# 128-row matmuls throughout the prompt's attention, and paged attention with late sums, split softmax steps and unnormalised exponentials of both maps

## The chip, the core and the metric

The program runs on one NeuronCore of a Trainium2 chip. The metric is the device time of one execution in microseconds (us). The engines are TensorE (PE in the rows; PEld is its weight load), VectorE (DVE), ScalarE (ACT), GpSimd (POOL) and SyncE (SP), which here only issues DMAs. Each engine runs its own queue in order; semaphores join them.

## What is computed

One decoder layer runs for a prompt of 1024 tokens behind 16 learned meta tokens, and for eight single-token samples with 4096 cached tokens each. Its attention is differential: four heads, each with two softmax maps of 64 columns over values of 128 columns, an ALiBi bias and causal masking. Beside it stands a convolution group of width 31. Both go into one output projection, and a SwiGLU network of 2816 hidden columns follows. Everything is float32.

```python
def diff_attend(q, k, v, q_pos, k_pos, lam, slopes):
    s = einsum('bqhjd,bkhjd->bhjqk', q, k) * HEAD_DIM ** -0.5
    s = s - slopes * (q_pos[:, None] - k_pos[None, :])
    s = where(k_pos <= q_pos, s, NEG_INF)
    p = softmax(s, axis=-1)
    a = p[:, :, 0] - lam * p[:, :, 1]
    return einsum('bhqk,bkhe->bqhe', a, v)
# sample: the same over cache_k[page_table], cache_v[page_table] (32 pages of 128
# tokens per sample) and the sample's own new key and value
```

## The kernel before

Products that must be exact are made of three matmuls (`mm3`, lines 147 to 149): each operand is split into a rounded part H and a remainder L, and HH, HL and LH are added in PSUM. The program is written as one stream, which a planner orders by priority on a simulated time line; the pools' buffers are given out by that planner, and an instruction waits for a buffer until its last reader is done.

*Prompt.* The input projection comes in stripes of 128 columns: the convolution's eight, then per head a stripe each of v, q and k (`stripe_v`, `stripe_q`, `stripe_k`), whose chunks are emitted between the attention blocks of the head before. `attn(h, i)` takes head h and query block i of 128 rows, over W = 16 + 128(i+1) keys. For each map j a score tile is made of two matmuls (lines 498 and 499): the first has 128 rows, with q's rounded 64 rows and their remainders stacked (`L1`) against k's rounded rows twice (`R1`); the second has q's rounded 64 rows against k's remainder `R2`, 64 rows. VectorE adds the bias and takes the maximum (line 500), ScalarE the exponential (508), VectorE combines the maps (516), TensorE transposes blocks (524), ScalarE copies them out (527), and TensorE multiplies by v (538). Key tile 0 holds the 16 meta tokens: its transpose has 16 columns and its product 16 rows (`vm`). The convolution runs on VectorE and GpSimd behind the first attention blocks. The tiles of 1056 columns (`slab`) share 35 buffers.

*Samples.* `dec_units` is a generator that is stepped at set points of the prompt's code, from block 3 of the attention on. A key unit loads two pages (`page_pair`, line 649, on SP), GpSimd multiplies them by the query (664), VectorE sums each 64 columns into the scores (668). A value unit loads two pages and multiplies them by the weights `a` on TensorE (716), four pages side by side in four column groups. Key units run ahead of value units by `lag`, and from then on two and two. When the 16 key units of a batch are out, `dec_softmax` follows at once: bias, maximum, an all-reduce over the partitions on GpSimd (686), subtraction, exponential, sum, a second all-reduce (692), reciprocal, scaling, and the two maps into one, `a` (700). `dec_values` begins with the sample's own value (706). The page tiles have four buffers of a tag `kv`, and after attention six more of a tag `p`, which then serve six of every seven pairs. Each page's DMA is placed in SP's queue behind the latest matmul of the prompt, by order alone.

```python
yield from keys(per + cfg["lag"])     # lag=2 key units ahead of the values
...
for b in range(DB):
    for n in dec_values(b, st):       # stops after each value unit
        yield
        yield from keys(n)            # as many key units after a group of value units
```

After attention comes the output projection, then the feed-forward network (`ffn`): gate and up (`pg`, `pu`) and down (`dn`, line 974 adds each of its 128x512 tiles into `y` on VectorE). Score, gate, up and down tiles share six PSUM buffers. `fill` steps the sample's work between those blocks. When the last values are out, `sample_units` sums the four column groups from `pvD` (line 1093) and runs the samples' output projection and feed-forward network.

Of the kernel before, what the change touches and what calls it, by code (L numbers as in the profile page):

```python
# [16 lines left out]
P = 128  # L17
# [28 lines left out]
def tile_layer(ctx: ExitStack, tc: tile.TileContext, I, O, cfg):  # L46
# [70 lines left out]
    pvD = dr.tile([DB, 4, NH, 512], F32, name="pvD")  # L117
# [166 lines left out]
    def stripe_k(h):  # L284
        HL = w_in_split(4 + h)
        R1s = [slab(f"R1_{h}{j}", F32R) for j in range(2)]
        R2 = slab(f"R2_{h}", F32R)
        k = slab(f"kT{h}")
        heads[h].update(R1=R1s, R2=R2)
# [29 lines left out]
    def stripe_v(h):  # L319
        HL = w_in_split(8 + h)  # L320
        vT = slab(f"vT{h}")
        for c, o in proj(HL, f"pv{h}"):
            key_evac(vT, o, c, 8 + h, "s")
            if c < 2:
                yield
        v = slab(f"V{h}")
        heads[h] = {"V": v}
        for pt, ts, name in key_tiles(vT, f"vn{h}"):
            for t0, nj, rows, c in key_runs(ts):
                dst = vm[:, h * P : (h + 1) * P] if t0 == 0 else v[:, (t0 - 1) * P : (t0 - 1 + nj) * P]  # L330
                S.copy(dst, pt[:rows, c * P : (c + nj) * P])
        D.dma_start(nvp[META:, h, :].rearrange("(j p) d -> p j d", j=NB), kn(v))
        yield

    def v_out():
        D.dma_start(nvp[0:META].rearrange("t h d -> t (h d)"), vm)
# [139 lines left out]
    def attn(h, i):  # L476
# [8 lines left out]
        L1s, R1s, R2 = heads[h]["L1"], heads[h]["R1"], heads[h]["R2"]  # L485
# [6 lines left out]
        for j in range(2):  # L492
            p = slp.tile([P, NKEY], F32, tag="p", name=f"p{h}{i}{j}", bufs=cfg["p"])
            sl = slice(j * HD, (j + 1) * HD)
            for a in range(0, W, w):
# [3 lines left out]
                T.matmul(o, lhsT=L1s[j][sl, qs], rhs=R2[sl, a:e], start=False, stop=True)  # L499
# [35 lines left out]
        for st, ts in ats:  # L535
            for n, t in enumerate(ts):
                w = KT[t][1]
                x = T.matmul(  # L538
                    o[:, oc], lhsT=st[:w, n * P : (n + 1) * P], rhs=vtile(h, t),
# [39 lines left out]
    mTs = cst.tile([P, 8, DB], F32, name="mTs")  # L579

# [74 lines left out]
    def dec_scores(b, st):  # L655
# [4 lines left out]
        for pg in range(0, NPG, 2):  # L660
            kt = page_pair(ck, b, pg, f"k{b}_{pg}")
            n = b * NPG // 2 + pg // 2
            eng = V if cfg["dve_mul"] and n % cfg["dve_mul"] == 0 else G
            eng.tensor_tensor(kt, kt, qB.unsqueeze(1).to_broadcast([P, 2, 512]), op=ALU.mult)  # L664
            for g in ((pg, pg + 1) if n < cfg["ksp"] else (slice(pg, pg + 2),)):
                src = kt if isinstance(g, slice) else kt[:, g - pg : g - pg + 1, :]
                g = g if isinstance(g, slice) else slice(g, g + 1)
                V.tensor_reduce(  # L668
                    s[:, g, :].rearrange("p a c -> p (a c)"),
                    src.rearrange("p a (c d) -> p (a c) d", d=HD), axis=AX.X, op=ALU.add,  # L670
                )
            yield b

    def dec_softmax(b, st):
# [7 lines left out]
        sv = s.rearrange("p g c -> p c g")  # L682
        m = smt(f"dm{b}", 8, 2)
        V.tensor_reduce(m, sv, axis=AX.X, op=ALU.max)
        mg = smt(f"dg{b}", 8, 2)
        G.partition_all_reduce(mg, m, P, bass.bass_isa.ReduceOp.max)
        V.tensor_tensor(s, s, mg.unsqueeze(1).to_broadcast([P, NPG + 1, 8]), op=ALU.subtract)
        S.activation(s, s, AF.Exp)
        l = smt(f"dl{b}", 8, 2)
        V.tensor_reduce(l, sv, axis=AX.X, op=ALU.add)  # L690
        lg = smt(f"dk{b}", 8, 2)
        G.partition_all_reduce(lg, l, P, bass.bass_isa.ReduceOp.add)
        co = smt(f"dc{b}", 8, 2)
        V.reciprocal(co, lg)
        cov = co.rearrange("p (h j) -> p h j", j=2)
        V.tensor_scalar(cov[:, :, 1], cov[:, :, 1], neglam, None, op0=ALU.mult)
        V.tensor_tensor(s, s, co.unsqueeze(1).to_broadcast([P, NPG + 1, 8]), op=ALU.mult)
        a = dec.tile([P, NPG + 1, NH], F32, tag="a", name=f"a{b}")
        s4 = s.rearrange("p g (h j) -> p (g h) j", j=2)
        V.tensor_tensor(a.rearrange("p g h -> p (g h)"), s4[:, :, 0], s4[:, :, 1], op=ALU.add)  # L700
        st[b] = a

    def dec_values(b, st):
        a = st.pop(b)
        pv = pdec(f"pv{b}")
        T.matmul(pv[0:NH, :], lhsT=a[:DB, NPG, :], rhs=nat["v"], start=True, stop=False)
        vs = []
        for pg in range(0, NPG, 2):
# [3 lines left out]
            if len(vs) == size:  # L712
                for q, vt in vs:
                    for i in range(2):
                        g = (q + i) % 4
                        x = T.matmul(  # L716
                            pv[32 * g : 32 * g + NH, :], lhsT=a[:, q + i, :], rhs=vt[:, i, :],
                            start=(q + i < 4 and g > 0), stop=q + i >= NPG - 4, tile_position=(0, 32 * g),
# [3 lines left out]
                vs = []  # L722
            yield 0 if vs else size
        pvs = dec.tile([P, 512], F32, tag="gs", name=f"pvs{b}", bufs=2)
        for g in range(4):
            S.copy(pvs[32 * g : 32 * g + NH, :], pv[32 * g : 32 * g + NH, :])
            D.dma_start(pvD[b, g], pvs[32 * g : 32 * g + NH, :])

    def dec_units():
        st = {}  # L730
        ks = (b for bb in range(DB) for b in dec_scores(bb, st))
        nk, ready = 0, 0
        per = NPG // 2

        def softmaxes():
            nonlocal ready
            while "k" in nat and ready < nk // per:
                dec_softmax(ready, st)
                ready += 1

        def keys(n):
            nonlocal nk
            for _ in range(n):
                if nk < DB * per:
                    next(ks)
                    nk += 1
                    softmaxes()
# [5 lines left out]
        softmaxes()  # L753
# [331 lines left out]
    def sample_units():  # L1085
        og = slab("og")
        og2 = slab("og2")
        for g in range(4):
            D.dma_start(
                (og, og2)[g // 2][:DB, (g % 2) * 512 : (g % 2) * 512 + 512].rearrange("b (h e) -> b h e", h=NH),  # L1090
                bass.AP(tensor=pvD.tensor, offset=pvD.offset + g * NH * 512, ap=[[4 * NH * 512, DB], [512 + P, NH], [1, P]]),
            )
        V.tensor_tensor(og[:DB, :1024], og[:DB, :1024], og2[:DB, :1024], op=ALU.add)
        o = og[:DB, 0:512]
        V.tensor_tensor(o, o, og[:DB, 512:1024], op=ALU.add)
# [243 lines left out]
    lag=2,  # L1339
# [46 lines left out]
```

## Time and profile before

| | us |
|---|---|
| median of three timed runs | 1557.42 (1555.67 to 1562.95) |
| the profiled execution | 1566.71 |
| its span, first to last instruction | 1564.9 |
| TensorE busy in the span | 1441.4 |
| VectorE, ScalarE, GpSimd busy | 932.0, 517.9, 561.9 |

In the profile a busy TensorE includes the time in which one matmul holds up the next; how far apart two of them start is read from the timeline. Behind an idle time stands what ended it; "issue" means that nothing of the profile was waited for. The granted clock of TensorE is 1 at 2.4 GHz and 0.5 at 1.2 GHz; a stretch shows the mean. In a matmul's row 64*128 is the weights' rows by columns, and behind it stand the moving rows and columns. Lines are those of the kernel before.

### The profile page before, as it was taken

What the parts mean: (1) busy time and instruction counts of PE and PEld (TensorE: products, weight loads), DVE (VectorE), ACT (ScalarE), POOL (GpSimd) and SP (SyncE); (2) the same over time, 40 slices, a digit from 0 to 9 for tenths busy, and PEclk for the clock granted to TensorE, in tenths of its full rate; (3) what the DMA queues carried; (4) which work ended last, traced back from release to release, by engine and by line L of the source; (5) the groups of instructions that cost most, each with busy time, mean ns of one, the idle gap of its engine ahead of it and who ended that gap; (6) DMA issues with size and microseconds to landing.
All of it is one profiled execution on the core that took longest, in us unless ns stands there. A gap on an engine that the chain in (4) does not pass through costs nothing.

```text
span 1564.9 us, 21652 instructions
## 1 busy us (share of the span) xinstructions
PE 1441.4 (92%) x6974; PEld 1080.5 (69%) x6974; DVE 932.0 (60%) x1519; ACT 517.9 (33%) x1023; POOL 561.9 (36%) x351
## 2 busy tenths in 40 slices
PE   6999999999869999989796996979979999999996
PEld 5998778888636787667474674756757677566665
DVE  5789987866545567565564745535545527454247
ACT  6566655586435334213112020111112121212121
POOL 3698735325224213444452533525445100000013
PEclk9999899999857999999898997999989999999999
DMA  8202113315405547668575664766767765764464
GB/s 261 60 12 57 37 58 95 108 59 166 142 0 168 185 152 248 202 215 270 184 250 173 202 215 157 242 195 205 240 189 232 238 219 178 262 200 142 155 210 163
DMA packets 199119, 264.03 MB, mean 169 GB/s; under 512 B 16119, under 2 KB 99384, under 8 KB 198997
## 3 DMA queue, kind: packets, MB, share of 16 engines
q1 hardware_dynamic: 199005, 262.64, 51.4%
q8 instruction: 55, 0.90, 0.2%
q14 instruction: 59, 0.48, 0.1%
HBM read 245.85 MB, written 17.22 MB: 168 GB/s over the span
## 4 chain that ended last, share of the span: by engine, by line
PE 74%; DVE 10%; issue 6%; DMA 4%; POOL 3%; SPq 2%; ACT 1%; POOLq 0%; DVEq 0%; ACTq 0%
PE pg L147 6%; PE pg L149 6%; PE pg L148 6%; PE pu L147 5%; PE pu L148 5%; PE pu L149 5%; PE pv L716 4%; PE dn L147 4%; PE dn L148 3%; PE dn L149 3%; PE o L538 3%; PE S L499 2%; PE mo L149 2%; PE mo L148 2%; PE mo L147 2%
## 5 line engine op out<-in xcount | busy, mean ns | idle before, releaser
L664 POOL TENSOR_TENSOR k<-k,qB 128x1024 f32<-128x1024 f32 x128 | 318.8, 2505 | 343.9 <-DMA k<-in_cache_k 247.3
L668 DVE TENSOR_REDUCE s<-k 128x16 f32<-128x1024 f32 x128 | 155.1, 1214 | 153.6 <-POOL k L664 153.5
L147 PE MATMUL dn<-wH,aH 128*128 128x512 f32 x352 | 144.3, 412 | 28.5 <-DVE y L974 28.5
L931 ACT CAST wH<-wr 128x1024 fp32r<-128x1024 f32 x66 | 69.2, 1048 | 300.0 <-DVE wL L933 151.9
L147 PE MATMUL pu<-hH,wH 128*128 128x512 f32 x352 | 141.3, 401 | 4.2 <-DVE y L972 4.2
L148 PE MATMUL dn<-wL,aH 128*128 128x512 f32 x352 | 143.8, 408 | 0.0
L149 PE MATMUL dn<-wH,aL 128*128 128x512 f32 x352 | 142.6, 405 | 0.0
L933 DVE TENSOR_TENSOR wL<-wr,wH 128x1024 fp32r<-128x1024 f32 x66 | 106.1, 1608 | 60.2 <-ACT wH L931 23.5
L147 PE MATMUL pg<-hH,wH 128*128 128x512 f32 x352 | 141.2, 401 | 0.0
L148 PE MATMUL pu<-hL,wH 128*128 128x512 f32 x352 | 140.7, 400 | 0.0
L149 PE MATMUL pu<-hH,wL 128*128 128x512 f32 x352 | 140.5, 400 | 0.0
L149 PE MATMUL pg<-hH,wL 128*128 128x512 f32 x352 | 139.9, 398 | 0.0
L148 PE MATMUL pg<-hL,wH 128*128 128x512 f32 x352 | 139.6, 397 | 0.0
L404 POOL TENSOR_TENSOR cb<-cb 128x512 f32<-128x512 f32 x80 | 101.8, 1305 | 21.2 <-ACT cb L403 12.1
L147 PEld LDWEIGHTS dn<-wH,aH 128*128 128x128 f32 x352 | 68.6, 195 | 59.1 <-DVE y L974 35.4
L974 DVE TENSOR_TENSOR y<-dn,y 128x512 f32<-128x512 f32 x144 | 95.9, 683 | 21.2 <-PE dn L149 20.8
L413 DVE SCALAR_TENSOR_TENSOR acc<-u,cw,acc 128x512 f32<-128x512 f32 x144 | 99.3, 749 | 0.3
L950 DVE TENSOR_TENSOR sg<-sg,pu 128x512 f32<-128x512 f32 x44 | 30.0, 682 | 107.6 <-PE pu L149 107.5
L147 PEld LDWEIGHTS pu<-hH,wH 128*128 128x128 f32 x352 | 67.1, 191 | 29.1 <-issue 11.9
L148 PEld LDWEIGHTS dn<-wL,aH 128*128 128x128 f32 x352 | 68.8, 195 | 25.5 <-issue 10.3
L147 PEld LDWEIGHTS pg<-hH,wH 128*128 128x128 f32 x352 | 66.4, 189 | 28.6 <-issue 12.5
L957 ACT CAST aH<-sg 128x512 fp32r<-128x512 f32 x44 | 27.3, 621 | 175.5 <-DVE sg L950 175.4
(571 smaller groups left out, 3008.8 us busy)
## 6 DMA issues: line engine op xcount, KB each, us to landing
k<-in_cache_k SPq DMA_DIRECT2D x256, 256.0 KB
v<-in_cache_v SPq DMA_DIRECT2D x256, 256.0 KB
wr<-in_w_gate SPq DMA_DIRECT2D x22, 512.0 KB
wr<-in_w_up SPq DMA_DIRECT2D x22, 512.0 KB
wr<-in_w_down SPq DMA_DIRECT2D x22, 512.0 KB
sd<-in_w_down SPq DMA_DIRECT2D x22, 512.0 KB
sw_gate<-in_w_gate SPq DMA_DIRECT2D x20, 512.0 KB
sw_up<-in_w_up SPq DMA_DIRECT2D x20, 512.0 KB
```

What stands on the lines that cost most here:

```text
L147: T.matmul(out, lhsT=wH, rhs=xH, start=first, stop=False)
L148: T.matmul(out, lhsT=wH, rhs=xL, start=False, stop=False)
L149: mark(T.matmul(out, lhsT=wL, rhs=xH, start=False, stop=last))
L404: G.tensor_tensor(accp, accp, t, op=ALU.add)
L413: V.scalar_tensor_tensor(dst, src, cw[:, ct, k : k + 1], acc, op0=ALU.mult, op1=ALU.add)
L538: x = T.matmul(o[:, oc], lhsT=st[:w, n * P : (n + 1) * P], rhs=vtile(h, t), start=t == 0, stop=t == nt - 1,)
L664: eng.tensor_tensor(kt, kt, qB.unsqueeze(1).to_broadcast([P, 2, 512]), op=ALU.mult)
L668: V.tensor_reduce(s[:, g, :].rearrange("p a c -> p (a c)"), src.rearrange("p a (c d) -> p (a c) d", d=HD), axis=AX.X, op=ALU.add,)
L716: x = T.matmul(pv[32 * g : 32 * g + NH, :], lhsT=a[:, q + i, :], rhs=vt[:, i, :], start=(q + i < 4 and g > 0), stop=q + i >= NPG - 4, tile ...
L931: S.copy(H[:, :1024], raw[:, :1024])
L933: V.tensor_tensor(L[:, :1024], raw[:, :1024], H[:, :1024].bitcast(F32), op=ALU.subtract)
L974: V.tensor_tensor(y[b][:, ws], o, y[b][:, ws], op=ALU.add)
```

## The change

Prompt: `R2` becomes two tiles of 128 rows, the key's remainder stacked twice, so that the second score matmul has 128 rows: it multiplies all of `L1`, and so adds the product of both remainders too. VectorE writes the second half of each. Key tile 0 is transposed 128 columns wide, its 16 rows are copied into one of three tiles whose other rows are zero, and `vm` has 128 rows, zero below the 16th.

Samples: a key unit's sum is emitted behind the product of the next key unit (`rlag`; an order, no semaphore). The softmax is split: bias, maximum and one all-reduce when the batch's sums are out (`dec_max`), subtraction and exponential two key units later (`dec_exp`, `elag`), sums over the pages amid the values (`dec_total`). The exponentials are not divided by their sums; both maps go to the value matmuls as eight columns. The sums over partitions, the reciprocals, the sample's own value and the difference of the maps follow once for all batches in `sample_units`. `lag` is 7 instead of 2.

```diff
     def stripe_k(h):
-        R2 = slab(f"R2_{h}", F32R)
+        R2s = [slab(f"R2_{h}{j}", F32R) for j in range(2)]
...
-                (G if cfg["r2_g"] else V).tensor_tensor(R2[sl, d], k[sl, d], R1s[j][sl, d].bitcast(F32), op=ALU.subtract)
+                (G if cfg["r2_g"] else V).tensor_tensor(R2s[j][sl, d], k[sl, d], R1s[j][sl, d].bitcast(F32), op=ALU.subtract)
+                V.tensor_tensor(R2s[j][ot, d], k[sl, d], R1s[j][sl, d].bitcast(F32), op=ALU.subtract)
...
-    vm = cst.tile([META, AW], F32, name="vm")
+    vm = cst.tile([P, AW], F32, name="vm")
+    G.memset(vm, 0.0)
+    metas = [cst.tile([P, P], F32, name=f"metaT{x}") for x in range(3)]
+    for x in metas:
+        G.memset(x, 0.0)
...
-                T.matmul(o, lhsT=L1s[j][sl, qs], rhs=R2[sl, a:e], start=False, stop=True)
+                T.matmul(o, lhsT=L1s[j][:, qs], rhs=R2s[j][:, a:e], start=False, stop=True)
...
-                k0, w = KT[t]
-                T.transpose(out=pt[:w, n * P : (n + 1) * P], in_=A[:, k0 : k0 + w], identity=ident)
+                k0 = KT[t][0]
+                T.transpose(out=pt[:, n * P : (n + 1) * P], in_=A[:, k0 : k0 + P], identity=ident)
...
-                S.copy(st[:rows, c * P : (c + nj) * P], pt[:rows, c * P : (c + nj) * P])
+                dst = metas[(h * NB + i) % 3][:rows, :] if t0 == 0 else st[:rows, c * P : (c + nj) * P]
+                S.copy(dst, pt[:rows, c * P : (c + nj) * P])
...
-                    o[:, oc], lhsT=st[:w, n * P : (n + 1) * P], rhs=vtile(h, t),
+                    o[:, oc], lhsT=metas[(h * NB + i) % 3] if t == 0 else st[:, n * P : (n + 1) * P], rhs=vtile(h, t),
...
     def dec_scores(b, st):
-            eng.tensor_tensor(kt, kt, qB.unsqueeze(1).to_broadcast([P, 2, 512]), op=ALU.mult)
-            for g in ((pg, pg + 1) if n < cfg["ksp"] else (slice(pg, pg + 2),)):
-                V.tensor_reduce(s[:, g, :]..., src..., axis=AX.X, op=ALU.add)
+            x = G.tensor_tensor(kt, kt, qB.unsqueeze(1).to_broadcast([P, 2, 512]), op=ALU.mult)
+            products.append((s[:, pg : pg + 2, :], kt))
+            if len(products) > cfg["rlag"]:
+                head_sums(x)
...
+    def head_sums(after):
+        s, kt = products.pop(0)
+        x = V.tensor_reduce(
+            s.rearrange("p a c -> p (a c)"), kt.rearrange("p a (c d) -> p (a c) d", d=HD), axis=AX.X, op=ALU.add
+        )
+        if after is not None:
+            tc.add_manual_dep(x.ins, after.ins.name, behind, reason="sums behind a later product")
...
+    def dec_exp(b, st):
+        s, mg = st[b]
         V.tensor_tensor(s, s, mg.unsqueeze(1).to_broadcast([P, NPG + 1, 8]), op=ALU.subtract)
         S.activation(s, s, AF.Exp)
-        V.tensor_reduce(l, sv, axis=AX.X, op=ALU.add)
-        G.partition_all_reduce(lg, l, P, bass.bass_isa.ReduceOp.add)
-        V.reciprocal(co, lg)
-        V.tensor_scalar(cov[:, :, 1], cov[:, :, 1], neglam, None, op0=ALU.mult)
-        V.tensor_tensor(s, s, co.unsqueeze(1).to_broadcast([P, NPG + 1, 8]), op=ALU.mult)
-        V.tensor_tensor(a.rearrange("p g h -> p (g h)"), s4[:, :, 0], s4[:, :, 1], op=ALU.add)
+        st[b] = s
+
+    def dec_total(b, s):
+        V.tensor_reduce(dsum[:, b, :], s.rearrange("p g c -> p c g"), axis=AX.X, op=ALU.add)
+        V.tensor_tensor(selfa, selfa, s[:DB, NPG, :], op=ALU.add)
...
     def dec_values(b, st):
-        T.matmul(pv[0:NH, :], lhsT=a[:DB, NPG, :], rhs=nat["v"], start=True, stop=False)
-                            pv[32 * g : 32 * g + NH, :], lhsT=a[:, q + i, :], rhs=vt[:, i, :],
+                            pv[32 * g : 32 * g + 8, :], lhsT=a[:, q + i, :], rhs=vt[:, i, :],
...
+            if pg == NPG // 2:
+                dec_total(b, a)
...
+        def softmaxes(all_=False):
+            while "k" in nat and ready < (nk - len(products)) // per:
+                dec_max(ready, st)
+                at.append(nk)
+                ready += 1
+            while exped < ready and (all_ or nk >= at[exped] + cfg["elag"]):
+                dec_exp(exped, st)
+                exped += 1
...
     def sample_units():
+        ogs = [slab(f"og{g}") for g in range(4)]        # eight DMAs from pvD
+        tot = pdec("dtot")
+        T.matmul(tot[:DB, : DB * 8], lhsT=ones, rhs=dsum.rearrange("p b c -> p (b c)"), start=True, stop=True)
+        V.tensor_tensor(mine, tot..., own, op=ALU.mult)
+        V.tensor_reduce(co, mine..., axis=AX.X, op=ALU.add)
+        V.reciprocal(co, co)
+        for g in range(1, 4):
+            V.tensor_tensor(o2, o2, ogs[g][:DB, :1024], op=ALU.add)
+        for j in range(2):                              # own value, sum, scaling: 512 columns each
+            V.tensor_tensor(t, nat["v"]..., w..., op=ALU.mult)
+            V.tensor_tensor(hv(ogs[0], j), hv(ogs[0], j), t, op=ALU.add)
+            V.tensor_tensor(hv(ogs[0], j), hv(ogs[0], j), cov[:, :, j]..., op=ALU.mult)
...
-    lag=2,
+    lag=7, rlag=1, elag=2,
```

## Rows read from the trace of the kernel before

**Rows 1.** Page, part 1: busy time of each engine.
```profile
PE 1441.4 (92%) x6974; PEld 1080.5 (69%) x6974; DVE 932.0 (60%) x1519; ACT 517.9 (33%) x1023; POOL 561.9 (36%) x351
```

**Rows 2.** Stretches: busy PE, PEld, DVE, ACT, POOL; granted TensorE clock, DMA share, GB/s.
```profile
150.00:200.00 50.00, 41.02 (x198) 35.17 (x197) 48.74 (x97) 32.02 (x69) 40.03 (x33) 0.85 0.11 32
200.00:400.00 200.00, 194.41 (x1134) 165.48 (x1134) 148.69 (x348) 125.63 (x319) 79.19 (x54) 0.97 0.30 94
400.00:505.00 105.00, 85.62 (x325) 55.29 (x324) 49.97 (x155) 44.38 (x111) 30.84 (x18) 0.66 0.33 110
505.00:1240.00 735.00, 673.48 (x3001) 483.10 (x3000) 419.88 (x500) 159.90 (x266) 287.43 (x139) 0.95 0.64 209
```

**Rows 3.** Waits of TensorE: us in total, times, longest.
```profile
PE dn L147 <- DVE y L974: 28.5, 8, 7.6
PE pv L706 <- DVE a L700: 28.4, 4, 13.9
PE S L498 <- DVE mx L500: 14.7, 4, 10.2
```

**Rows 4.** Timeline of TensorE in attention: start, us, what.
```profile
282.12 0.40 PE L498 MATMUL S<-R,L 128*128 128x328 f32 x1
282.45 0.41 PE L499 MATMUL S<-R,L 64*128 64x328 f32 x1
...
289.02 0.34 PE L149 MATMUL pq<-xH,wi2L 128*128 128x384 f32 x1
289.20 0.34 PE L147 MATMUL pq<-xH,wi2H 128*128 128x384 f32 x1
...
414.82 0.70 PE L499 MATMUL S<-R,L 64*128 64x400 f32 x1
415.45 0.70 PE L498 MATMUL S<-R,L 128*128 128x400 f32 x1
...
500.22 0.48 PE L538 MATMUL o<-vm,ats 16*128 16x128 f32 x2
500.63 0.94 PE L538 MATMUL o<-V,ats 128*128 128x128 f32 x6
```

**Rows 5.** Timeline of GpSimd around one all-reduce.
```profile
855.13 0.43 POOL L692 PARTITION_ALL_REDUCE dk<-dl  x1 [5.91 <-issue]
862.63 9.56 POOL L664 TENSOR_TENSOR k<-k,qB 128x1024 f32<-128x1024 f32 x4 [7.07 <-issue]
```

**Rows 6.** Waits of VectorE: us in total, times, longest.
```profile
DVE s L668 <- POOL k L664: 153.5, 53, 12.1
...
DVE dc L694 <- POOL dk L692: 32.2, 7, 12.6
```

**Rows 7.** Score matmuls of 64 rows (line 499) in two stretches.
```profile
400.00:414.00 14.00, 5.80 (x14) 2.66 (x14) 0.99 0.32 96
414.00:499.00 85.00, 16.24 (x25) 6.84 (x24) 0.58 0.33 111
```

**Rows 8.** VectorE groups with two SBUF inputs: by form; durations min/median/max.
```profile
L876 DVE TENSOR_TENSOR mL<-mx,mH 128x384 fp32r<-128x384 f32 x8 | 6.6, 828 | 6.7 <-ACT mH L875 6.7
...
L700 DVE TENSOR_TENSOR a<-s x8: 286/291/2508, 449.1 to 1234.6; 128x132 f32<-128x132 f32 x8
```

**Rows 9.** Group of line 706.
```profile
L706 PE MATMUL pv<-natv,a 8*4 8x512 f32 x16 | 11.5, 809 | 28.4 <-DVE a L700 28.4
```

**Rows 10.** Waits of the DMA queue on SP: us in total, times, longest.
```profile
SPq L649 <- DVE s L668: 67.8, 14, 14.7
...
SPq L130 <- PE S L499: 36.5, 2, 22.0
```

**Rows 11.** Timeline of VectorE at the sample's first sum.
```profile
1284.31 1.21 DVE L1093 TENSOR_TENSOR og<-og,og 8x1024 f32<-8x1024 f32 x1 [7.18 <-DMA og<-pvD]
```

**Rows 12.** GpSimd group of the key products, 505 to 1240.
```profile
L664 POOL TENSOR_TENSOR k<-k,qB 128x1024 f32<-128x1024 f32 x108 | 271.3, 2527 | 308.2 <-DMA k<-in_cache_k 218.5 <-issue 62.9 <-DMA v<-in_cache_v 10.5
```

More of the change, by code (lines that the diff above doesn't have):

```diff
@@ L116, in tile_layer @@
     qsD = dr.tile([DB, AW], F32, name="qsD")
[L117 removed]
+    pvD = dr.tile([DB, 4, 8, 512], F32, name="pvD")
     def rstd_of(ssq, rows, inv_n, name, w=1, add=EPS):
@@ L579, in tile_layer @@
     mTs = cst.tile([P, 8, DB], F32, name="mTs")
+    selfa = cst.tile([DB, 8], F32, name="selfa")
+    G.memset(selfa, 0.0)
+    dsum = cst.tile([P, DB, 8], F32, name="dsum")
+    ones = cst.tile([P, DB], F32, name="ones")
+    G.memset(ones, 1.0)
+    own = cst.tile([DB, DB, 8], F32, name="own")
+    G.memset(own, 1.0)
+    G.affine_select(
+        out=own, in_=own, pattern=[[-1, DB], [0, 8]], compare_op=ALU.is_equal, fill=0.0, base=0, channel_multiplier=1
+    )
     def dec_consts():
@@ L716, in dec_values @@
                         x = T.matmul(
-                            pv[32 * g : 32 * g + NH, :], lhsT=a[:, q + i, :], rhs=vt[:, i, :],
-                            start=(q + i < 4 and g > 0), stop=q + i >= NPG - 4, tile_position=(0, 32 * g),
+                            pv[32 * g : 32 * g + 8, :], lhsT=a[:, q + i, :], rhs=vt[:, i, :],
+                            start=q + i < 4, stop=q + i >= NPG - 4, tile_position=(0, 32 * g),
                         )
@@ L731, in dec_units @@
         ks = (b for bb in range(DB) for b in dec_scores(bb, st))
-        nk, ready = 0, 0
+        nk, ready, exped, at = 0, 0, 0, []
         per = NPG // 2
[L735 to L738, printed above, removed]
+        def softmaxes(all_=False):
+            nonlocal ready, exped
+            while "k" in nat and ready < (nk - len(products)) // per:
+                dec_max(ready, st)
+                at.append(nk)
                 ready += 1
+            while exped < ready and (all_ or nk >= at[exped] + cfg["elag"]):
+                dec_exp(exped, st)
+                exped += 1
         def keys(n):
@@ L746, in keys @@
                     nk += 1
-                    softmaxes()
+                    if nk == DB * per:
+                        while products:
+                            head_sums(None)
+                    softmaxes(nk == DB * per)
                     yield
@@ L1094, in sample_units @@
-        o = og[:DB, 0:512]
-        V.tensor_tensor(o, o, og[:DB, 512:1024], op=ALU.add)
+            for j in range(2):
+                D.dma_start(
+                    ogs[g][:DB, j * 512 : j * 512 + 512].rearrange("b (h e) -> b h e", h=NH),
+                    bass.AP(
+                        tensor=pvD.tensor, offset=pvD.offset + (g * 8 + j) * 512,
+                        ap=[[4 * 8 * 512, DB], [2 * 512 + P, NH], [1, P]],
+                    ),
+                )
+        tot = pdec("dtot")
@@ new lines, in sample_units @@
+        T.matmul(tot[:DB, : DB * 8], lhsT=ones, rhs=dsum.rearrange("p b c -> p (b c)"), start=True, stop=True)
+        mine = smt("dmine", DB * 8, 1)[:DB].rearrange("p (b c) -> p b c", b=DB)
+        V.tensor_tensor(mine, tot[:DB, : DB * 8].rearrange("p (b c) -> p b c", b=DB), own, op=ALU.mult)
+        co = smt("dco", 8, 1)[:DB]
+        V.tensor_reduce(co, mine.rearrange("p b c -> p c b"), axis=AX.X, op=ALU.add)
+        V.reciprocal(co, co)
+        cov = co.rearrange("p (h j) -> p h j", j=2)
@@ new lines, in sample_units @@
+        V.tensor_scalar(cov[:, :, 1], cov[:, :, 1], neglam[:DB], None, op0=ALU.mult)
+        o2 = ogs[0][:DB, :1024]
+        for g in range(1, 4):
+            V.tensor_tensor(o2, o2, ogs[g][:DB, :1024], op=ALU.add)
+        hv = lambda t, j: t[:DB, j * 512 : j * 512 + 512].rearrange("b (h e) -> b h e", h=NH)
+        for j in range(2):
+            t, w = hv(ogs[1], j), selfa.rearrange("p (h j) -> p h j", j=2)[:, :, j]
+            V.tensor_tensor(
+                t, nat["v"].rearrange("b (h e) -> b h e", h=NH), w.unsqueeze(2).to_broadcast([DB, NH, P]), op=ALU.mult
+            )
+            V.tensor_tensor(hv(ogs[0], j), hv(ogs[0], j), t, op=ALU.add)
+            V.tensor_tensor(
+                hv(ogs[0], j), hv(ogs[0], j), cov[:, :, j].unsqueeze(2).to_broadcast([DB, NH, P]), op=ALU.mult
+            )
@@ L1096, in sample_units @@
+        o = ogs[0][:DB, 0:512]
+        V.tensor_tensor(o, o, ogs[0][:DB, 512:1024], op=ALU.add)
         ov = o.rearrange("b (h e) -> b h e", h=NH)
```

44 lines of the change are left out of this document (12 added, 32 removed).

## The prediction

> **What bounds the kernel now.** I read the page first, then a table of busy time over stretches, then TensorE's waits, and only then the timeline. TensorE is busy for 92% of the span [rows 1], so its time is what counts, but the stretches differ [rows 2]. From 150 to 200 VectorE is busy for 48.7 of 50 us and TensorE for 41: the convolution's taps bound it. From 200 to 400 TensorE is busy for 194 of 200 us. From 400 to 505, the end of attention, it is busy for 85.6 of 105 us at a mean granted clock of 0.66. From 505 to 1240, the feed-forward network with the paged attention beside it, it idles for 735 - 673.5 = 61.5 us at a mean clock of 0.95. The list of waits names VectorE at each large idle time [rows 3]: `dn` blocks wait for `y` sums (28.5 us), the value matmuls for the weights `a` (28.4), a score matmul for a row maximum (10.2 of 14.7 in one wait).
>
> Two things lie beneath. In attention a score matmul of 328 columns with 128 rows is followed 0.33 us later by its partner of 64 rows; two projection matmuls of 384 columns, all with 128 rows, stand 0.18 us apart at the same full clock, 2.4 GHz [rows 4]. So a change of row count between neighbours costs about as much again as the matmul. In the paged part GpSimd stands idle for 5.91 us before an all-reduce and for 7.07 us before the product after it, though neither waits for data [rows 5]. VectorE's queue is in order, so it stands behind that: 153.5 us for products, 32.2 for the second all-reduce of a batch [rows 6].
>
> **128 rows everywhere.** There are 112 pairs of score matmuls: 25 between 414 and 499, mostly at 1.2 GHz [rows 7], the other 87 mostly at 2.4. Full clock: 0.33 us apart now; 328 columns without the change of rows are 0.18 x 328/384 = 0.15; 174 x 0.18 = 31 us. Half clock: 0.63 apart for 400 columns, twice 0.18 without, so 50 x 0.28 = 14 us. The 16-row meta pair holds TensorE for 0.41 us [rows 4]; a plain matmul of 128 columns is at most the 0.18 of 384 and at least its third, 0.06; I take 0.12, so 32 blocks x 0.17 = 5 us. Together 50 us of TensorE time. The 16-column transposes become 128 wide, 32 x 0.06 = 2 us at most by the same ends; I take 0.
>
> What of this is on the path? Between 150 and 200 nothing, VectorE sets the end there. Between 200 and 400 lie about 60 pairs and 18 blocks, 22 + 3 = 25 us, but VectorE's 148.7 us stand close behind. It gets the new subtractions, six a head, 24 in all. The nearest form, `mL`, 384 columns and two SBUF inputs, takes 0.83 us on the mean [rows 8]. So 18 x 0.83 = 15 us come here, and VectorE stands at 164 of the 175 us that TensorE would leave. I take 16 of the 25. The six subtractions of head 0 fall where VectorE is the bound: +5. The ends for all 24: the 132-column add of `a` takes 0.29 us on the median and 2.51 at most, beside products of 2.4 [rows 5, 8]: 7 and 60 us.
>
> The Trainium skill's SBUF — State Buffer (section "SBUF: two separate sides") speaks against this edit: a VectorE instruction with two SBUF inputs and a GpSimd instruction shut each other out for the whole instruction. The slowest add of `a` agrees. If each of the 24 subtractions met a product of 2.4 us, the rule would add 58 us to the sum; by the row's median it adds nothing.
>
> **The end of attention, 400 to 505.** 14 pairs at full clock, 25 at half and eight meta pairs: 28 x 0.18 + 50 x 0.28 + 8 x 0.3 = 21 us, of which I count 15, as a block here also waits for its own maximum, exponential and transposes. The stall of 10.2 us goes with the all-reduce that is removed: -10. The first one stays, and batch 0's exponential is emitted straight after it, so its stall stays. The clock: 2 x (1 - 0.66) x 105 = 71 us at half clock. Less idle time (19) and the gaps counted above (14), some 38 us of work would take 19 less at full clock. TensorE was in the row-changing score matmuls when the clock fell: full at 289, half at 414 [rows 4]. I count half, -10 (ends 0 and -19). Sum: -35.
>
> **Paged attention, 505 to 1240.** Removed: a batch's second all-reduce, the reciprocal and scaling, `a`, the small matmul with `natv`. Added: eight value rows for four (the same 512 columns streamed: 0), sums one product late, the exponential two key pairs late, keys seven pairs ahead of values for two. (1) The weights are then the exponential itself, four key pairs old when the first value matmul needs it: the 28.4 us go. (2) Each batch stops GpSimd once, not twice, for 5.9 + 7.1 = 13 us. The products behind it are late by that, but VectorE reads a sum only after the next product was due. Six score buffers of PSUM let `dn` run ahead by 6 blocks x 6 x 0.23 = 8 us (0.23: 512 columns at the 384-column pace), so a delay of VectorE below that doesn't reach TensorE. Of the 33 us of waits for `y` (61.5 - 28.4) I leave 11: -22. (3) Clock: 2 x 0.05 x 735 = 73 us at half clock; if half of the idle time lies in it, 42 us of work lose 21; I count 16 back. (4) The `natv` matmuls are 16 instructions of 0.8 us with little overlap in pairs, about 1 us a batch: -8 [rows 9]. (5) Against it: a key buffer is held one product longer. SP already waits 67.8 us for sums to free one, 14.7 at most [rows 10], and value pages and weights are queued behind. No value matmul has waited for a page so far. I charge 1.5 us for each of 7 batches, +10. Sum: -28 - 22 - 16 - 8 + 10 = -64.
>
> **The rest.** Before the sample's output projection VectorE gets three 8x1024 adds for one and eight operations of 512 columns more, 2 x 1.21 + 8 x 0.6 = 7 us in one burst [rows 11], partly under the 8 us of PSUM lead: +4 (0 to 7). Four more small DMAs of `pvD` stand in SP's queue with them: 0, at worst inside the same 7. The memsets at the start run while the first rows load: 0.
>
> Sum: +5 - 16 - 35 - 64 + 4 = -106. The profiled run took 1566.7 us (span 1564.9), 9.3 above the median of the timed runs, 1557.4. So 1461 for a run like the profiled one and **1451** for the median.
>
> **Rivals.** (a) *Attention gives nothing*: less work on TensorE only uncovers VectorE, or one more buffer per head (35 slabs in all) blocks the next head's loads. For it: VectorE at 164 of 175; SP already waits 22 us at a time for a score matmul to free a slab [rows 10]. Against it: TensorE was busy for 97% of 200 to 400. The 16, the 15 and the clock's 10 are lost: 1451 + 41 = 1492. (b) *The page ring takes the place of the wait removed*: keys held longer, SP stuck behind them during the 13 us stop, value pages late. At 6 us more a batch, 7 x 6 = 42: 1493. For it: 14 waits of SP on sums now. Against: no matmul waits for a page. (c) *Full clock through attention*: the gaps count wholly (25 for 16, 21 for 15), the clock term is 19, no wait for `y` is left (11): 1451 - 9 - 6 - 9 - 11 = 1416. For it: the clock fell in a stretch without idle time. (d) *The spacing is not the rows' doing* but another property of the score matmuls, such as both adding into one bank. Projections do that too, at 0.18 [rows 4], which speaks against it. The 16, 15 and 10 are gone: 1492.
>
> The Trainium skill, TensorE: Matmul & The Clock Gate, section "Why this matters for your kernels", says that a single matmul with 32 rows takes the time of one with 128, and advises to place few rows side by side. By it alone (d) would hold; for neighbours of unlike row counts the trace doesn't bear it out.
>
> (e) *Slower*: the ring of key and value buffers paces the whole paged part. A buffer comes round again after seven page pairs. About 216 pairs are left there (108 key products [rows 12], as many values), 735/216 = 3.4 us a pair, a turn of 24 us. If a buffer's life passes that, every pair is late by a seventh of the excess, and weights and values with it. To end 8 us above now takes 124 us in the place of the 10 charged, 0.57 us a pair, a life of 28 us. One product later is two pairs, 7 us, so it decides only if the life is 21 now; at a life of 29, 0.71 a pair, 154 us: 1595. SP's 14 waits among 108 products speak against it.
>
> **Chances.** Forecast 0.55 (its own range 1425 to 1478), (a) 0.15, (b) 0.12, (c) 0.10, (d) 0.03, (e) 0.05. The range reaches to (c) and over (a), (b) and (d), 1408 to 1512, and leaves out some 0.2 with the tails. Half a per cent, 8 us, is about what a measurement of this kernel can tell from no change. Faster by more: all but (e) and a tail of (a) and (b), 0.93; within it 0.03; slower 0.04.
>
> **What the new profile should show.** Score matmuls of 328 columns 0.15 us apart at full clock; one all-reduce a batch with 6 and 7 us around it; no wait for `a`; waits for `y` below 15 us; VectorE's wait for products below 60; the clock from 400 to 505 above 0.8. Wrong would be: value matmuls that wait for pages, SP waiting on sums for over 150 us, VectorE full from 200 to 400.

## The result, and the profile after

The changed kernel took 1494.0 us (median of four runs, 1485.7 to 1502.4) beside 1560.2 us for the kernel before (four runs): a ratio of 0.957, 95% interval 0.950 to 0.965. The profiled execution took 1499.5 us, span 1497.7, which stands beside the 1461 forecast for a run like the profiled one. The four runs spread over 17 us, so a kernel that differs from this one by less than some 10 us isn't told from it by its time alone. One run of the seventh kernel below took 7454.9 us and is left out of its numbers.

The page's busy time of each engine, and the same stretches as in [rows 2], after:

```profile
PE 1376.2 (92%) x6960; PEld 1069.6 (71%) x6960; DVE 950.2 (63%) x1531; ACT 511.5 (34%) x1019; POOL 559.0 (37%) x351
```

```profile
150.00:200.00 50.00, 38.02 (x205) 35.40 (x206) 49.42 (x93) 30.21 (x65) 34.90 (x29) 0.83 0.11 33
200.00:400.00 200.00, 170.91 (x1091) 161.18 (x1090) 162.05 (x360) 116.19 (x306) 84.98 (x55) 0.93 0.33 102
400.00:505.00 105.00, 75.79 (x418) 64.39 (x417) 77.62 (x185) 53.40 (x140) 44.92 (x25) 0.80 0.42 137
505.00:1240.00 735.00, 710.64 (x3261) 514.26 (x3262) 424.30 (x513) 165.39 (x265) 266.85 (x126) 0.98 0.69 226
```

From 200 to 400 TensorE is busy for 171 us where it was busy for 194 [rows 2], and idle for the other 29; VectorE has risen from 149 to 162. TensorE's two longest waits in that stretch are for VectorE's maxima and combined maps, where before no wait there was over 1.4 us in total:

```profile
PE AT L528 <- DVE mx L504: 5.7, 3, 3.8
PE AT L528 <- DVE p L520: 4.8, 2, 4.2
```

From 505 to 1240 TensorE's idle time has gone from 61 to 24 us and its clock from 0.95 to 0.98.

Fixed windows shift against the work when a kernel gets faster, so the same pieces of work are compared too. The marks are the first matmul of the attention's output projection `mo`, the first gate matmul `pg` of the feed-forward network, the first `pg` of its 16th of 22 weight blocks, and the end of the last `dn` matmul. The windows between them (the first from 150 us on), before and after:

```profile
150.00:505.20 355.20, 321.25 (x1655) 256.14 (x1653) 247.61 (x597) 202.03 (x498) 150.26 (x103) 0.86 0.28 90
602.10:1247.90 645.80, 584.66 (x2588) 411.38 (x2587) 362.42 (x403) 125.81 (x175) 266.15 (x119) 0.94 0.66 216
1247.90:1552.40 304.50, 303.89 (x1443) 204.68 (x1441) 141.80 (x208) 60.34 (x101) 21.65 (x20) 1.00 0.58 195
```

```profile
150.00:489.40 339.40, 269.12 (x1638) 249.17 (x1638) 282.27 (x620) 194.34 (x491) 160.84 (x105) 0.87 0.31 99
585.80:1174.50 588.70, 567.99 (x2600) 405.47 (x2599) 346.13 (x378) 126.41 (x175) 251.01 (x108) 0.98 0.72 238
1174.50:1489.50 315.00, 307.31 (x1429) 206.15 (x1427) 152.47 (x228) 61.24 (x104) 24.72 (x21) 0.99 0.55 185
```

Attention ends 16 us earlier (489.4 for 505.2), the paged part is 57 us shorter (588.7 for 645.8), the tail 10.5 longer (315.0 for 304.5); what stands after the last `dn` shrinks from 12.5 to 8.2, and the output projection stays (96.9 and 96.4). Together 67 us, the difference of the spans. So attention gave a third of its forecast, while TensorE's work in it fell by 52 us: its idle time there rose from 34 to 70.

TensorE's waits that answer to [rows 3], and VectorE's that answer to [rows 6], after:

```profile
PE S L502 <- DVE mx L504: 16.8, 7, 5.0
PE dn L147 <- DVE y L996: 10.9, 4, 7.4
...
PE pv L729 <- DMA v<-in_cache_v: 5.5, 6, 2.6
```

```profile
DVE s L687 <- POOL k L677: 139.7, 43, 8.3
...
DVE s L709 <- POOL dg L704: 48.6, 8, 7.5
```

The waits for `a` are gone, those for `y` are 10.9 us. A little waiting for value pages is new. VectorE still waits 139.7 us for products, so the forecast "below 60" failed, yet TensorE hardly feels it. The pieces of the mechanism, in TensorE's and GpSimd's timelines:

```profile
291.63 0.38 PE L542 MATMUL o<-vm,metaT 128*128 128x128 f32 x2
291.85 0.61 PE L542 MATMUL o<-V,ats 128*128 128x128 f32 x4
...
298.28 0.34 PE L502 MATMUL S<-R,L 128*128 128x392 f32 x1
298.45 0.34 PE L503 MATMUL S<-R,L 128*128 128x392 f32 x1
298.64 0.34 PE L502 MATMUL S<-R,L 128*128 128x392 f32 x1
```

```profile
878.12 0.39 POOL L704 PARTITION_ALL_REDUCE dg<-dm  x1 [7.99 <-issue]
886.05 10.89 POOL L677 TENSOR_TENSOR k<-k,qB 128x1024 f32<-128x1024 f32 x4 [7.54 <-issue]
```

Score matmuls of 392 columns now stand 0.17 to 0.19 us apart, where 328 columns with a change of rows stood 0.33 apart [rows 4]. One stop of GpSimd a batch is left, and it is no shorter than before [rows 5]. (A stop is the idle time around an all-reduce and the all-reduce itself.)

### The profile page after: what moved, and what is told of

It is laid out like the page before. It is cut to its first block, busy times and chain, and to the rows that moved or that the text cites. A ratio compares the mean times of both kernels' runs of the same rounds, so it can differ in the third digit from the quotient of the medians.

```text
span 1497.7 us, 21649 instructions
## 1 busy us (share of the span) xinstructions
PE 1376.2 (92%) x6960; PEld 1069.6 (71%) x6960; DVE 950.2 (63%) x1531; ACT 511.5 (34%) x1019; POOL 559.0 (37%) x351
## 4 chain that ended last, share of the span: by engine, by line
PE 50%; DVE 16%; DMA 9%; SPq 9%; issue 8%; ACT 5%; POOL 3%; DVEq 0%; POOLq 0%; ACTq 0%
SPq L663 4%; PE pg L147 4%; PE pg L149 4%; PE pg L148 4%; SPq L657 4%; DMA k<-in_cache_k 3%; PE pu L147 3%; PE pu L149 3%; PE pu L148 3%; PE dn L147 3%; PE dn L148 3%; PE dn L149 3%; PE pv L729 2%; POOL k L677 2%; DVE s L687 2%
## 5 line engine op out<-in xcount | busy, mean ns | idle before, releaser
L687 DVE TENSOR_REDUCE s<-k 128x16 f32<-128x1024 f32 x128 | 155.0, 1213 | 139.7 <-POOL k L677 139.7
L147 PE MATMUL dn<-wH,aH 128*128 128x512 f32 x352 | 142.4, 408 | 12.5 <-DVE y L996 10.9
L1068 POOL TENSOR_TENSOR y<-y,wfpost 128x512 f32<-128x512 f32 x10 | 17.4, 1758 | 207.3 <-ACT ft L1066 207.1
L147 PEld LDWEIGHTS pg<-hH,wH 128*128 128x128 f32 x352 | 66.1, 188 | 27.3 <-issue 10.7
L149 PEld LDWEIGHTS dn<-wH,aL 128*128 128x128 f32 x352 | 67.7, 192 | 22.9 <-issue 7.7
```

The costliest lines, as they stand in the source:

```text
L147: T.matmul(out, lhsT=wH, rhs=xH, start=first, stop=False)
L149: mark(T.matmul(out, lhsT=wL, rhs=xH, start=False, stop=last))
L687: x = V.tensor_reduce(s.rearrange("p a c -> p (a c)"), kt.rearrange("p a (c d) -> p (a c) d", d=HD), axis=AX.X, op=ALU.add)
```

## Experiments

Two questions were open. Where did attention's share go? Theories: VectorE's queue, with 24 more subtractions in it, took the place of TensorE's row changes; or the new slabs hold the loads back; or the saving was never there. And what gave the paged part its 57 us: the removed stop of GpSimd, the late sums, or the late exponential? Kernels that ran side by side share their runs of the kernel before. "End of attention" is the first `mo` matmul, "paged part" the second window above, "tail" the third.

**The halves by themselves.** The first kernel is the kernel before with the prompt's edits only:

```diff
+                V.tensor_tensor(R2s[j][ot, d], k[sl, d], R1s[j][sl, d].bitcast(F32), op=ALU.subtract)
```

> The kernel before with the prompt's part of the change alone (128 rows everywhere). In the profile of the whole change the first matmul of the output projection stands at 489.4 us for 505.2 before, so attention gave 16 us where the prediction had 46. Theory A, VectorE's queue is what attention now waits for: this part alone gives 5 to 12 us (the second all-reduce and its 10 us stall are still there), some 1548 us against 1558, ratio 0.993, and TensorE's waits for VectorE between 200 and 400 grow from 4 us to over 15. The prediction's own sizes: 5 - 16 - 25 = -36 us, ratio 0.977.

1576.1 us, ratio 1.011 (1.009 to 1.013): slower, where both expectations had a gain. Its windows:

```profile
150.00:501.10 351.10, 271.27 (x1646) 250.07 (x1645) 275.59 (x622) 198.00 (x496) 152.55 (x102) 0.85 0.28 91
598.60:1254.10 655.50, 583.46 (x2590) 409.00 (x2589) 356.99 (x403) 125.91 (x175) 267.60 (x119) 0.93 0.65 212
```

TensorE's work up to the end of attention falls by exactly the forecast 50 us (321.3 to 271.3), but the end moves by 4: idle time takes the rest, and VectorE is busy for 28 us more. The paged part is 10 longer, with 40.3 us of waits for `a` where [rows 3] has 28.4.

The second has the paged edits only (late sums, split softmax, eight value rows):

```diff
-    lag=2,
+    lag=7, rlag=1, elag=2,
```

> The kernel before with the samples' part alone (late sums, split softmax, unnormalised exponentials, lag 7), 64-row and 16-row matmuls kept. If the parts add up, this one gives what the whole gave less the prompt's share: 66 - 8 = 58 us, ratio 0.963, with 50 us of it after the first output projection matmul. The prediction's sizes: -10 - 64 + 4 = -70 us, ratio 0.955. If the two parts help each other (TensorE denser, clock higher), it gives less than 50, ratio over 0.968.

1494.1 us, ratio 0.958 (0.955 to 0.961): all of the change's gain.

```profile
150.00:490.10 340.10, 316.38 (x1644) 258.17 (x1643) 261.98 (x599) 197.92 (x496) 161.95 (x106) 0.87 0.31 99
586.90:1170.10 583.20, 565.61 (x2599) 402.92 (x2598) 345.24 (x378) 126.52 (x175) 252.92 (x108) 0.99 0.73 240
```

Attention ends at 490.1 as in the whole change, with TensorE 47 us busier. So the 16 us that attention gained are the paged edits', and the 128 rows as built bring nothing beside them.

**VectorE's load in attention.** In the third kernel the second half of each `R2` is zero, written by GpSimd (it leaves out the product of the two remainders, as the kernel before does):

```diff
+        for j in range(2):
+            G.memset(R2s[j][(1 - j) * HD : (2 - j) * HD, :NKEY].bitcast(F32), 0.0)
-                V.tensor_tensor(R2s[j][ot, d], k[sl, d], R1s[j][sl, d].bitcast(F32), op=ALU.subtract)
```

> The whole change, but the second half of each R2 tile is set to zero by GpSimd when the tile is given out, where VectorE wrote the remainder there; the product of the two remainders is so left out of the scores, as in the kernel before. TensorE's work, its 128 rows and the number of slabs stay. VectorE loses 24 subtractions, 19.5 us. Theory A (VectorE sets the pace of attention): the first output projection matmul comes 8 to 18 us earlier than 489.4, and the time is 8 to 18 us below the changed kernel's 1494, ratio to before 0.945 to 0.952. Rival B (one more slab per head blocks the loads): no change, ratio 0.957.

1485.2 us, ratio 0.953 (0.951 to 0.954). In the fourth the subtractions are made twice:

```diff
                 V.tensor_tensor(R2s[j][ot, d], k[sl, d], R1s[j][sl, d].bitcast(F32), op=ALU.subtract)
+                V.tensor_tensor(R2s[j][ot, d], k[sl, d], R1s[j][sl, d].bitcast(F32), op=ALU.subtract)
```

> The whole change with each of VectorE's 24 new subtractions made twice, to the same place: 19.5 us more of VectorE's work in attention, nothing else. Theory A: 10 to 20 us later than the changed kernel, ratio to before 0.963 to 0.970, first output projection matmul at 500 to 509. Rival B: under 4 us, 0.957 to 0.960.

1516.7 us, ratio 0.973 (0.970 to 0.976). VectorE's groups of the subtractions, in the fourth:

```profile
L300 DVE TENSOR_TENSOR R<-kT,R 64x384 fp32r<-64x384 f32 (+1 forms) x24 | 22.6, 943 | 0.7
L299 DVE TENSOR_TENSOR R<-kT,R 64x384 fp32r<-64x384 f32 (+1 forms) x24 | 19.4, 810 | 0.7
```

A second set of 22.6 us moves the end of attention from 489.4 to 509.0, by 19.6, as expected. VectorE's busy time up to there rose by only 10.3 us (282.3 to 292.6), since some of its other operations took less, so busy time alone doesn't set the end. Without the subtractions (third kernel) attention ends at 484.1, only 5.3 earlier where 8 to 18 were expected. That is no more than the end moves without any edit in attention: the paged edits alone end it at 490.1, and at 483.7 with six empty steps far behind it (the last kernel below). So more work for VectorE is paid for, but that less of it gains anything isn't shown.

The tenth kernel asks what 128 rows are worth at equal load of VectorE: the paged edits, the 64-row matmuls, and the same 24 subtractions into a tile that nothing reads.

```diff
+        R2b = [slab(f"R2b_{h}{j}", F32R) for j in range(1)] * 2
+                V.tensor_tensor(R2b[j][ot, d], k[sl, d], R1s[j][sl, d].bitcast(F32), op=ALU.subtract)
```

> The samples' part alone (64-row and 16-row matmuls kept), and VectorE makes the 24 subtractions of the whole change, into a tile that nobody reads. TensorE's work is that of 64 rows and VectorE's that of 128. If VectorE alone sets attention's pace, the first output projection matmul stands where it stands in the whole change, 489 to 493, and the ratio stays 0.957. If TensorE was the bound at 64 rows and VectorE became it by the subtractions, so that both together cost more than either: 495 to 510, ratio 0.961 to 0.970.

1524.5 us, ratio 0.979 (0.976 to 0.982). Its window up to the end of attention:

```profile
150.00:516.70 366.70, 320.27 (x1638) 258.02 (x1638) 282.79 (x621) 197.68 (x497) 161.21 (x105) 0.86 0.29 92
```

VectorE is as busy as after the change (282.8 and 282.3 us), TensorE 51 us busier, and attention ends 27 us later, later than either expectation. Beside the second and third kernels (490.1 and 484.1, both without subtractions) the rows are worth 6, no more than the spread just named. The subtractions cost the 64-row kernel 26.6 us and the 128-row kernel 5.3. Why these differ so much isn't settled. The extra tile may weigh in the tenth: SP stands for 40.1 us there at weights whose tile a score matmul must free, for 17.9 in the second and 1.0 in the changed kernel; that this reaches TensorE isn't shown.

The eleventh is the third with the page keys begun at the last block of attention, not at the fourth:

```diff
-    vgrp=2, fing=5, ml_g=0, fend=22, cst=0, db=3, cn=6, scn=12, wo0=27, wor=2, c0=7,
+    vgrp=2, fing=5, ml_g=0, fend=22, cst=0, db=31, cn=6, scn=12, wo0=27, wor=2, c0=7,
```

> The kernel with zero halves, but the samples' key units start at the last attention block and not at the fourth. Some 23 products of GpSimd and sums of VectorE (28 us) leave attention; the paged part, which holds them later, grows, so the total tells little. Read is the first output projection matmul: theory A (VectorE still sets the pace at 484): 465 to 475. If the blocks' own chains from engine to engine set it: 478 to 486.

1478.3 us (two runs), ratio 0.949 (0.945 to 0.952). The window up to the end of attention, and the paged part:

```profile
150.00:437.00 287.00, 246.52 (x1627) 234.12 (x1628) 211.13 (x566) 196.96 (x494) 107.95 (x86) 0.93 0.20 65
531.20:1129.60 598.40, 559.65 (x2534) 405.59 (x2533) 361.70 (x395) 124.93 (x172) 288.43 (x123) 0.98 0.71 234
```

With 51 us less on VectorE than in the third kernel (211.1 for 262.3 us), 57 less on GpSimd (108.0 for 165.1) and the granted clock at 0.93 for 0.87, attention ends at 437.0, 47 us earlier, more than was expected. The page keys' work beside attention is what held it back. Most comes back: TensorE then waits 27.2 us for value pages, and 31 us (1442.9 to 1474.2) lie after the last `dn` where 8 did.

**GpSimd's stop, and the lags.** The fifth kernel puts a second all-reduce back whose result nobody reads:

```diff
+        lg = smt(f"dk{b}", 8, 2)
+        G.partition_all_reduce(lg, dsum[:, b, :], P, bass.bass_isa.ReduceOp.add)
```

> The whole change with a second all-reduce put back for each batch, amid its values, on the sums over its pages; nobody waits for its result, and it changes no output. GpSimd so stops twice a batch again, 13 us each time, but VectorE waits for neither and the value matmuls don't either. Theory P, what reached TensorE before was the delay of the products behind GpSimd's stops: 20 to 35 us come back, ratio to before 0.970 to 0.979. Theory W, it was VectorE waiting at the all-reduces themselves, with the weights behind it: under 8 us come back, ratio under 0.963 (the changed kernel has 0.957).

1540.6 us, ratio 0.989 (0.987 to 0.991): 47 us lost against the change (41 between the profiled runs), more than either theory had. Attention ends at 505.7, where it ended before the change, and the paged part takes 614.2 us. Waits of TensorE and of the DMA queue on SP:

```profile
PE oT L569 <- DVE oh L561: 21.3, 2, 12.8
PE S L502 <- DVE mx L504: 20.3, 10, 5.9
PE pv L731 <- DMA v<-in_cache_v: 19.0, 6, 8.3
...
SPq L663 <- DVE s L687: 59.5, 14, 14.4
```

In attention it is a small operation of attention itself that stood behind the stop: GpSimd makes `or` (line 559), from inputs that VectorE had finished at 455.8, but comes to it at 468.8, and VectorE's `oh` and TensorE's transposes wait for it:

```profile
456.70 0.43 POOL L717 PARTITION_ALL_REDUCE dk<-dsum  x1 [5.76 <-DVE mx L504]
...
468.77 1.05 POOL L559 TENSOR_TENSOR or<-t,mhalf 128x4 f32<-128x4 f32 x1
469.85 3.23 DVE L561 SCALAR_TENSOR_TENSOR oh<-oh,or,subln 128x128 f32<-128x128 f32 x4 [12.48 <-POOL or L559]
```

In the paged part TensorE's waits for value pages (19.0 us, 5.5 in the changed kernel) and SP's for sums (59.5 us over the run, 33.9 in the changed kernel) fit the reading that products late behind a stop make sums late, and so page buffers and pages. The stops are not what was expected, though. Only two of the eight added all-reduces stand alone, with 13 us around them; six come right behind the first one, in the same stop:

```profile
911.28 0.40 POOL L704 PARTITION_ALL_REDUCE dg<-dm  x1 [7.18 <-issue]
913.40 0.41 POOL L717 PARTITION_ALL_REDUCE dk<-dsum  x1 [1.72 <-DVE selfa L715]
```

There GpSimd waits 1.7 to 2.9 us more, for VectorE's sums. So the 47 us are not the price of eight separate stops.

The sixth and seventh set one lag each to zero.

```diff
-    lag=7, rlag=1, elag=2,
+    lag=7, rlag=1, elag=0,
```

> The whole change with the subtraction and the exponential emitted straight behind the all-reduce (elag 0 for 2). VectorE stands before the subtraction until GpSimd's 6 us are over, once a batch. Theory W: 5 to 7 us of VectorE's time a batch, of which the PSUM lead covers most: 5 to 15 us come back, ratio 0.960 to 0.967. Theory P: nothing, 0.957.

1492.6 us, ratio 0.959 (0.956 to 0.962): no difference from the change that these runs could tell.

```diff
-    lag=7, rlag=1, elag=2,
+    lag=7, rlag=0, elag=2,
```

> The whole change with each sum emitted right behind its own product (rlag 0 for 1). Theory P: VectorE stands at the sum of the first product behind each stop of GpSimd, 7 to 13 us a batch, and y sums behind it: 15 to 30 us come back, ratio 0.967 to 0.976, waits of dn for y over 20 us. Theory W: a stop of 13 us is mostly covered by the 8 us lead that PSUM gives, under 8 us, 0.957 to 0.962.

1521.2 us (the middle of three runs, 1514.9 to 1528.2), ratio 0.978 (0.972 to 0.983). In the profiled runs it is 21 us longer than the change: attention ends 5.7 later, the output projection takes 5.5 more and the paged part 10.7 more (599.4). So the sums made one product late are worth 20 to 30 us.

**The tail.** In the changed kernel the queue on SP, and TensorE behind it:

```profile
1202.15 0.40 SPq L943 DMA_DIRECT2D wr<-in_w_down  x1
1224.47 0.40 SPq L1159 DMA_DIRECT2D swo<-in_w_out  x1
...
1230.76 0.46 SPq L945 DMA_DIRECT2D wr<-in_w_up  x1
```

```profile
1248.27 0.79 PE L149 MATMUL pu<-hH,wL 128*128 128x512 f32 x1 [4.00 <-DVE wL L955]
```

SP stands for 22 us at a load of `swo`, whose buffer waits for the sample's output projection, which waits for the new normalisation on VectorE. Weights of the feed-forward network are queued behind it and arrive late. The eighth kernel lets six pieces of other work pass first:

```diff
+        for _ in range(6):
+            yield
         mix = slab("smix")[:DB, :DM]
```

> The whole change with six empty steps between the samples' normalised attention output and their output projection, so that its loads are issued some 15 us later. In the changed kernel SP stands for 22 us at the fifth of those loads, until the first of the matmuls has freed a buffer, and two feed-forward weights behind it come after TensorE wants them (7.6 us idle, 6.8 us at half clock after 1175, where the kernel before had 0.6 and 0). If that is the cause, the weights come in time: 6 to 11 us less, ratio 0.950 to 0.953, idle time after the 480th gate matmul below 3 us. If the stretch is longer because it now holds more of the samples' matmuls, nothing changes: 0.957.

1484.4 us, ratio 0.952 (0.948 to 0.957). Its tail:

```profile
1169.20:1471.70 302.50, 300.90 (x1429) 203.63 (x1427) 145.75 (x224) 61.17 (x104) 21.13 (x21) 1.00 0.57 193
```

302.5 us for 315.0, idle for 1.6 us and at full clock: the tail's loss is gone. (SP still stands 27.8 us at that load, but weights are ahead of it now. The 480th gate matmul of the expectation is the mark of the third window, which has 720 before it.) The same holds in every trace: with the six steps the tail is 302.2 to 302.6 us in three kernels, without them 313.3 to 315.0 in all others that have the paged edits. Behind the last `dn` stand some 2 us more.

**Together.** The third and eighth edits at once:

> Both edits that gained, together: the second halves of R2 zero by GpSimd (the product of the two remainders left out, as in the kernel before), and the samples' output projection six steps later. If they work in different places, as theory A and the reading of SP's queue have it, they add: 8 + 8 us below the changed kernel, ratio 0.946 to 0.949. If the first gain was only luck of another order, 0.951 to 0.954.

1476.6 us, ratio 0.948 (0.946 to 0.950), the fastest here, 17.4 us below the changed kernel where the two edits by themselves gave 8.8 and 9.6. The tail's part is seen in the windows. The other part is not settled: in the profiled runs attention is 5.9 us shorter, which is within the spread named above, and the paged part 8.5, where neither edit has work. And the paged edits with the eighth, without the 128 rows:

> The samples' part alone with the same six steps, 64-row and 16-row matmuls kept. The samples' part alone had 0.958; the later loads should give 5 to 8 us here too, 0.953 to 0.955. Against the kernel with zero halves and later loads this tells what 128 rows are worth once VectorE doesn't pay for them: 0.004 to 0.008 by theory A, nothing if VectorE and the blocks' own chains bound attention either way.

1482.1 us, ratio 0.952 (0.949 to 0.955). Beside the ninth the rows without their subtractions come to some 5 us of the median, and the two intervals overlap. In the traces attention ends at the same time in both; the first matmuls of the output projection in the ninth and in this kernel:

```profile
L147 PE MATMUL mo<-wo4H,mH x16: 388/393/481, 483.5 to 568.0; 128*128 128x512 f32 x16
L147 PE MATMUL mo<-wo4H,mH x16: 391/394/475, 483.7 to 568.6; 128*128 128x512 f32 x16
```

So no gain of the 128 rows in attention is shown, with their subtractions or without.

## Why the prediction was right, and where it was wrong

**The total: inside the stated range, outside the forecast's own.** 1494 lies above 1425 to 1478. It is covered because the stated range, 1408 to 1512, was drawn over rivals (a), (b) and (d), which all gave 1492 or 1493 by different mechanisms; the total can't tell them apart, but the traces can. (d) is out: 392 columns stand 0.17 to 0.19 us apart. (b) is out: value matmuls wait 5.5 us for pages in all, and SP waits less for sums than before. (a), with a chance of 0.15, is nearest.

**Direction and paged part: right.** The term was -64 for 505 to 1240; the same work shrank by 57. The waits for `a` are gone, those for `y` are 10.9 us (11 forecast). The clock came back: 0.94 to 0.98 over the paged part. The +10 for the page ring was too much: SP's wait for sums fell from 67.8 [rows 10] to 33.9 us, and value matmuls wait 5.5. What was not foreseen is how much the removed stop itself is worth. The prediction priced the second all-reduce by who waits for it; the fifth kernel's have no reader and cost 47 us (41 between the profiled runs: 16 in attention and 25.5 in the paged part), through the work queued behind them. The exponential's lag, which was meant to end the waits for `a`, is worth nothing that could be measured by itself; the lag of the sums is worth 20 to 30 us.

**128 rows: the saving right, its place on the path wrong.** TensorE's 50 us were sized exactly (321.3 to 271.3 in the first kernel), and so were the 24 subtractions: 0.83 us each by [rows 8], 0.81 measured, 19.5 in all. The Trainium skill's SBUF — State Buffer (section "SBUF: two separate sides") would have added 58 us if each had met a product; in the changed kernel's trace none is seen held up by one. The longest of the 24, 2.68 us, agrees with the rule itself: it ran beside another GpSimd operation of 2.36 us (`wi1L`). But their sum stayed at the row's. The step that failed is "VectorE stands at 164 of the 175 us that TensorE would leave. I take 16 of the 25", and after it the 15 and the 10 of 400 to 505. That step counts TensorE's saving as time so long as VectorE's busy time stays below TensorE's. VectorE came out at 162 us and TensorE at 171, and still the rows made attention no shorter than the paged edits alone do (489.4 and 490.1): the time freed on TensorE became idle time (34 us up to the end of attention before, 70 after), part of it waits for VectorE. In the fourth kernel still more work for VectorE is paid for nearly whole. But VectorE's load is not the one bound: without the subtractions attention still ends at the same time with 64 rows as with 128 (483.7 and 483.5, the last kernel and the ninth). What does hold attention back is the page keys' work beside it (eleventh kernel). Rival (a) had the lost saving and its time, 1492, though by a partly different sum: attention gave 16 us where (a) leaves 5, the paged part 57 for 64, the tail lost 10.5 for 4, and what follows the last `dn` got 4.3 shorter. Its other half, the slabs, wasn't tried by itself.

**The removed stall in attention: right in kind.** 10 us were forecast; with the paged edits alone the end of attention moved by 15. The fifth kernel gives back 16, by another path: before, VectorE stood at the all-reduce's result, there it stands at `or` behind the all-reduce.

**The clock from 400 to 505: borderline.** 0.80 for 0.66 in the fixed window, which now holds 16 us of the output projection; over all of attention 0.87 for 0.86. TensorE's row changes are gone and the granted clock still falls; in the eleventh kernel, where TensorE idles less (40 of 287 us for 70 of 339), it is 0.93.

**The tail: mechanism wrong, size small.** +4 was charged for VectorE's burst against the lead in PSUM. The 10.5 us come from SP standing at one load, with weights behind it; with the load issued later the tail's loss is gone (302.5 us).

**Open.** `lag` and the unnormalised exponentials were not varied by themselves, so what ended the waits for `a`, and what part of the paged part's 57 us each of them brings, isn't shown. Why the prompt's edits alone lengthen the paged part by 10 us: the longer waits for `a` are shown, not what put them there. Which of VectorE's queue, GpSimd and the page loads holds attention most in the eleventh kernel's comparison: that edit moves all three. That edit was not made with 64 rows, so what the rows would gain once that work is gone is open.

## What to carry to other kernels

A saving on the busiest engine is worth what the next engine lets through: before counting it, add what the change puts on that engine, and don't take it for granted because that engine's busy time is still the smaller one (here, with VectorE at 162 of 200 us, TensorE's saving of 52 us up to the end of attention became idle time). An operation that stops a queue costs what is queued behind it, waiter or not. A load that must wait for a buffer belongs behind the weights in its DMA queue, and a change of several parts is worth taking apart: here one half gave all of the gain.

## What was not expected of the hardware

Eight all-reduces without a reader cost 47 us. In the changed kernel GpSimd stands idle for 5.8 to 8.7 us before one and 6.9 to 8.4 after it, though in most cases nothing that the profile shows is late. In the fifth kernel a second all-reduce right behind the first has no such idle time between the two (1.7 to 2.9 us in six of eight batches, put down to VectorE's sums): two of them side by side share one stop. The meta pair, now with 128 rows, holds TensorE for 0.22 us in the row shown (0.12 taken, 0.41 before [rows 4]).
